# The down product of a feed-forward by token instead of by channel, with the residual, the last norm and the output in the same order

## The chip, the cores and the metric

The kernel runs on one core of one Trainium2 chip. The metric is the device time of one execution in microseconds, as the median of several runs. The engines are TensorE (PE; its weight loads are PEld), VectorE (DVE), ScalarE (ACT), GpSimd (POOL) and SyncE (SP), whose queue issues nearly all DMAs. All arithmetic is float32; products of matrices are made from high and low parts in float32r.

## The reference

Two transformer blocks of 256 tokens and 1024 channels follow each other. The first has a convolution, a differential attention and a mixture of 32 experts, the second four mixers, a cross attention to a memory and a feed-forward with a short convolution. What concerns the change is the end:

```python
def conv_ffn(xn, w_up, w_conv, w_down):
    u = causal_depthwise_conv(xn @ w_up, w_conv)
    a, g = jnp.split(u, 2, axis=-1)
    return (a * jax.nn.silu(g)) @ w_down
...
        h = h + conv_ffn(rms_norm_2(h, g_ffn[l]), w_up[l], w_ffconv[l], w_down[l])
    return rms_norm_2(h, g_final)
```

`rms_norm_2` divides each token by the root of the mean square over its channels and multiplies by a gain for each channel. `w_up` is 1024 x 5632, `w_down` 2816 x 1024; 2816 is 22 blocks of 128 (`NFF`).

## The kernel before

The residual stream `xT` lies in SBUF with channels in the partitions: 8 tiles of 128 channels by 256 tokens. Weights come from HBM in loads of 1 MB into slots of 8 KB a partition (21 in all) and are split, block by block, into a high part (ScalarE, L364) and a low part (VectorE, L367). A product is then three (`mm3`, L453 to L458): high by high, high by low, low by high. Blocks are used in one written order (`self.blocks`), split up to `AHEAD` + 1 = 4 blocks ahead and loaded up to 12 loads ahead. The program is issued in the order of the Python code (`manual_schedule`): work beside the main run of products stands in generators (`spawn`), each of which takes a step whenever `tick` is called after a block.

The feed-forward (`feed_forward`, L1982) goes over the 22 blocks j. `raise_` (L2021) makes the two up products of block j, 24 products of 256 columns each. `gated` (L1994) then scales by the norm, convolves, gates and splits the result into high and low parts, in steps. `lower` (L2031) makes the down product of block j - 5 (`LAG`): the weights are the stationary operand, the gated values of 256 tokens the moving one, for each of 8 tiles of 128 output channels. The sums over all blocks stay in four PSUM banks (`acc`), two tiles to a bank. The last two blocks are taken together, tile by tile, so that `residual` (L2054) can add tiles to `xT` and square them while others are still being summed. Behind the last product come the sums of squares over the partitions as products with a column of ones (`stat`, L418), three Newton steps for the reciprocal root (`rsqrt`, L401), a diagonal matrix of it (L432) and a product with ones that spreads it to all partitions (L2083), then the multiplication of the output (L2085) and four stores from SP's queue (L2086). The gain has been put in before by ScalarE (L2080). The output is written as channels by tokens and transposed on the host.

Products with 512 moving columns exist elsewhere: `projN` (L492) has the activations of 128 tokens as stationary operand and 512 columns of weights moving, with the same `mm3`. Transposes on TensorE exist too (L1664 and others).

## Time and profile before

| | |
|---|---|
| runs, us | 1077.84, 1075.33, 1077.87; median 1077.84 |
| the profiled execution | span 1075.6 us, 2.2 under the median; the profile gives no other time for it |
| TensorE busy | 917.5 us (85%) |
| VectorE, ScalarE busy | 517.0 us (48%), 341.5 us (32%) |
| DMA | 301.14 MB, mean 280 GB/s |
| chain that ended last | PE 39%, DMA 38% (the experts' weights), DVE 2%, ACT 1% |
| feed-forward's down products | 528 of the 6250 products |

A busy share is taken over the whole span, and the stages differ: the experts' stage in the middle follows the loads, the stages before and after follow TensorE. Matmuls overlap in the profile, so the time of a product in a run of them is the distance from start to start and not its duration. The granted clock is the TensorE clock that the chip allows, as a share of full speed.

### The profile page before, as it was taken

Reading aid. Unit: us, or ns where it says so; the run is one execution under the profiler, and the core shown is the slowest. Engines: PE = TensorE matmul, PEld = TensorE weight load, DVE = VectorE, ACT = ScalarE, POOL = GpSimd, SP = SyncE. Lnnn points to the kernel's source line nnn. Section 1 sums busy time; section 2 is a strip of 40 time slices with the busy share of each in tenths; the row PEclk is TensorE's granted clock in tenths of the full one; section 3 lists DMA queues with packets and bytes.
Section 4 is the critical chain, followed back from the end, with each engine's and each line's share of the span. In section 5 each row is a group of like instructions: output and inputs, shape, how many; then the busy total and the mean of one; then the engine's idle time right before and its main releaser. Section 6 shows DMA issues by size and latency. Waiting matters only on the chain.

```text
span 1075.6 us, 15338 instructions
## 1 busy us (share of the span) xinstructions
PE 917.5 (85%) x6250; PEld 657.8 (61%) x6251; DVE 517.0 (48%) x1144; ACT 341.5 (32%) x614; POOL 1.2 (0%) x12
## 2 busy tenths in 40 slices
PE   6989989978766867667766995999999999999996
PEld 6759989734220403122210730688899899999995
DVE  6999978501110100001010020648486489878885
ACT  5326555201020101000000011554464465544453
POOL 0000000000000000000000000000000000000000
PEclk9999999989696878787796997998999999999998
DMA  9726556859999999999999999942365295453001
GB/s 368 294 78 232 201 191 248 301 225 420 420 418 420 421 420 418 420 420 419 419 420 421 420 418 422 394 161 100 119 211 184 90 363 209 169 185 118 2 1 40
DMA packets 45006, 301.14 MB, mean 280 GB/s; under 512 B 4864, under 2 KB 8320, under 8 KB 9088
## 3 DMA queue, kind: packets, MB, share of 16 engines
q1 hardware_dynamic: 44640, 299.58, 70.4%
q8 instruction: 51, 0.84, 0.3%
q10 hardware_dynamic: 288, 0.50, 0.2%
q14 instruction: 27, 0.22, 0.1%
HBM read 299.02 MB, written 1.05 MB: 279 GB/s over the span
## 4 chain that ended last, share of the span: by engine, by line
PE 39%; DMA 38%; DVE 2%; ACT 1%; issue 0%; DVEq 0%; SPq 0%; ACTq 0%
DMA slot<-in_we_dram 38%; PE ps L456 10%; PE ps L457 10%; PE ps L458 10%; PE ps L467 1%; PE ps L1384 1%; PE ps L1473 1%; PE ps L1956 1%; PE ps L1505 1%; PE ps L1922 1%; PE ps L1489 0%; PE ps L1738 0%; DVE slot L367 0%; PE ps L1735 0%; PE ps L420 0%
## 5 line engine op out<-in xcount | busy, mean ns | idle before, releaser
L456 PE MATMUL ps<-slot,slot 128*128 128x256 f32 (+1 forms) x1020 | 304.9, 299 | 0.4 <-DVE k L1797 0.4
L457 PE MATMUL ps<-slot,slot 128*128 128x256 f32 (+1 forms) x1020 | 297.6, 292 | 0.8 <-DVE slot L367 0.8
L458 PE MATMUL ps<-slot,slot 128*128 128x256 f32 (+1 forms) x1020 | 297.3, 292 | 0.2 <-DVE slot L367 0.2
L1505 PE MATMUL ps<-slot,k 128*32 128x512 f32 x1024 | 171.6, 778 | 77.5 <-DMA slot<-in_we_dram 77.5
L456 PEld LDWEIGHTS ps<-slot,slot 128*128 128x128 f32 x1020 | 196.6, 193 | 11.8 <-issue 7.3
L457 PEld LDWEIGHTS ps<-slot,slot 128*128 128x128 f32 x1020 | 196.8, 193 | 5.5 <-DVE slot L367 1.8
L367 DVE TENSOR_TENSOR slot<-slot,slot 128x1024 fp32r<-128x1024 f32 x159 | 191.9, 1217 | 14.2 <-ACT slot L364 14.2
L458 PEld LDWEIGHTS ps<-slot,slot 128*128 128x128 f32 x1020 | 196.7, 193 | 3.1 <-DVE slot L367 0.4
L364 ACT ACTIVATE slot<-slot 128x1024 fp32r<-128x1024 f32 x159 | 163.6, 1047 | 23.7 <-PE ps L458 17.7
L1505 PEld LDWEIGHTS ps<-slot,k 128*32 128x32 f32 x1024 | 26.3, 121 | 213.2 <-DMA slot<-in_we_dram 176.9
L1489 PE MATMUL ps<-slot,k 128*32 128x512 f32 x512 | 64.9, 627 | 33.2 <-DMA slot<-in_we_dram 27.4
L1544 DVE TENSOR_TENSOR xT<-xT,ps 128x512 f32<-128x512 f32 x28 | 19.2, 687 | 118.3 <-PE ps L1542 118.3
L1513 DVE TENSOR_TENSOR k<-k,ps 128x512 f32<-128x512 f32 x8 | 5.5, 687 | 133.0 <-PE ps L1505 133.0
L1475 ACT ACTIVATE k<-ps 128x512 f32<-128x512 f32 x16 | 9.6, 597 | 173.7 <-PE ps L1473 173.7
L1489 PEld LDWEIGHTS ps<-slot,k 128*32 128x32 f32 x512 | 13.6, 111 | 76.7 <-DMA slot<-in_we_dram 40.8
L1512 DVE SCALAR_TENSOR_TENSOR k<-k,ps 128x512 f32<-128x512 f32 x8 | 5.5, 687 | 113.9 <-ACT k L1511 113.9
L1473 PEld LDWEIGHTS ps<-k,slot 128*128 128x128 f32 x256 | 38.8, 243 | 27.2 <-issue 25.2
L1473 PE MATMUL ps<-k,slot 128*128 128x128 f32 x256 | 40.4, 330 | 16.3 <-DVE k L1406 8.6
L705 DVE SCALAR_TENSOR_TENSOR slot<-slot,params,slot 128x256 f32<-128x256 f32 x120 | 51.5, 477 | 0.0
L456 PE MATMUL ps<-k,slot 128*128 128x256 f32 x176 | 49.8, 283 | 0.0
L457 PE MATMUL ps<-k,slot 128*128 128x256 f32 x176 | 49.8, 283 | 0.0
L458 PE MATMUL ps<-k,slot 128*128 128x256 f32 x176 | 49.8, 283 | 0.0
(337 smaller groups left out, 931.3 us busy)
## 6 DMA issues: line engine op xcount, KB each, us to landing
slot<-in_we_dram SPq DMA_DIRECT2D x192, 1024.0 KB, 19.9
slot<-in_w_dram SPq DMA_DIRECT2D x47, 1024.0 KB, 5.2
slot<-in_wup_dram SPq DMA_DIRECT2D x22, 1024.0 KB, 5.3
slot<-in_wdn_dram SPq DMA_DIRECT2D x11, 1024.0 KB, 4.9
slot<-in_wkv_dram SPq DMA_DIRECT2D x8, 1024.0 KB, 19.9
xT<-in_xT_dram SPq DMA_DIRECT2D x2, 512.0 KB, 5.9
slot<-in_w_dram SPq DMA_DIRECT2D x2, 512.0 KB, 7.6
slot<-in_mem_dram SPq DMA_DIRECT2D x1, 1024.0 KB, 5.0
```

The costliest lines, as they stand in the source:

```text
L364: self.nc.scalar.activation(hi, w, AF.Copy)
L367: self.nc.vector.tensor_tensor(lo, w, hi.bitcast(F32), OP.subtract)
L456: mm(out, l[0], r[0], start=start, stop=False, **kw)
L457: mm(out, l[0], r[1], start=False, stop=False, **kw)
L458: mm(out, l[1], r[0], start=False, stop=stop, **kw)
L467: self.nc.tensor.matmul(out, w[0][:, k, c], h[2][:, k, :], start=a, stop=z)
L705: stt(a, y[:, i, j : j + T], half_taps[:, i, j : j + 1], a, OP.mult, OP.add)
L1384: nc.tensor.matmul(outs[tt][:], self.mem[:, k, ts], w[0][:, j, :], **kw)
L1473: mm(pg[:, j * P : j * P + P], h2[:, tt, k * P : k * P + P], flat(oh, tt), start=tt == 0, stop=tt == 1)
L1489: mm(pd[n][32 * e : 32 * e + 32, :], hT[:, f * P + 32 * e : f * P + 32 * e + 32], t[:, 512 * e : 512 * e + 512], start=f == 0, stop=f == 3,)
L1505: mm(pgu[m][32 * e : 32 * e + 32, :], xg[k // 4][:, k % 4 * P + 32 * e : k % 4 * P + 32 * e + 32], t[:, 512 * e : 512 * e + 512], start=k ...
L1544: tt_(xflat[:, s], xflat[:, s], py[:], OP.add)
```

## The change

The down product changes its operands' roles. The gated values of 128 tokens are stationary and 512 columns of weights move; the four PSUM banks now hold two halves of tokens (`tt`) by two halves of channels (`c`). `products` makes for each block 2 x 2 triples. The residual is brought into the same order beforehand: `by_token`, spawned after the up product of block 5, transposes `xT` on TensorE in four groups of four tiles, and ScalarE copies each group into a slot (`xn`). For the last two blocks the products of token half 0 come first, then `ending(0)`, then those of half 1, then `ending(1)`. `ending` adds the residual, squares with an accumulator on ScalarE (so the sum over the channels is a number for each partition), adds two numbers, makes the Newton steps and multiplies by the reciprocal root and the gain at once. The gain is a row of 1024 in every partition now, an input of its own (`gfin`, 512 KB, loaded by SP at the start of the stage). Four stores of 256 KB go out, of each half one from SP's queue and one from ScalarE's. The output is tokens by channels; the column sums, the diagonal matrix, the spreading product and the host's transpose are gone. The rest of the diff is comments.

```diff
-        ("g_mix", 8), ("g_xa", 8), ("g_mem", 8), ("g_ffn2", 8), ("g_fin", 8), ("p_scale", 2),
+        ("g_mix", 8), ("g_xa", 8), ("g_mem", 8), ("g_ffn2", 8), ("p_scale", 2),
...
-    put("g_fin", chan(f["g_final_2"]))
...
+        "gfin": np.ascontiguousarray(np.broadcast_to(f["g_final_2"], (P, D))),
...
         xT = self.xT
         n = self.n_ffn
         h, rb = n.h, n.rb
-        acc = [self.bank() for _ in range(4)]
+        acc = [[self.bank() for _ in range(2)] for _ in range(2)]
         three = lambda a: a[:].rearrange("p (j t) -> p j t", j=2)
         fs = {}
...
                     ths.append(self.spawn(gated(j, pu), 1 if j == 0 else 0))
                 self.tick()
-        def lower(js, done=lambda i: None):
+        def take_pairs(js):
             ws, fh = [], []
             for j in js:
                 ws.append(self.next_block())
                 self.finish(ths[j])
                 fh.append(fs.pop(j))
-            for i in range(KT):
-                s = slice(i * P, i * P + P)
+            return ws, fh
+        def products(js, ws, fh, tt):
+            t = slice(tt * P, tt * P + P)
+            for c in range(2):
+                s = slice(c * 512, c * 512 + 512)
                 for j, (w, _), f in zip(js, ws, fh):
-                    self.mm3(
-                        acc[i // 2][:, i % 2 * T : i % 2 * T + T], (w[0][:, 0, s], w[1][:, 0, s]), (f[:, 0, :], f[:, 1, :]),
-                        j == 0 and i % 2 == 0, j == NFF - 1, skip_group_check=True,
-                    )
-                done(i)
-            for _, release in ws:
-                release()
+                    self.mm3(acc[tt][c][:], (f[:, 0, t], f[:, 1, t]), (w[0][:, 0, s], w[1][:, 0, s]), j == 0, j == NFF - 1)
+        def lower(j):
+            ws, fh = take_pairs([j])
+            for tt in range(2):
+                products([j], ws, fh, tt)
+            ws[0][1]()
             self.tick()
-        # the output's norm goes on beside the last products
-        total = self.t(self.sm, [P, T], "sq_sum", bufs=2)
-        st = self.bank()
-        sqs = {}
-        def residual(i):
-            if i % 2 == 0:
-                return
-            for k in (i - 1, i):
-                stt(xT[:, k, :], acc[k // 2][:, k % 2 * T : k % 2 * T + T], 0.5, xT[:, k, :], OP.mult, OP.add)
-                sqs[k] = self.k1() if k else total
-                act(sqs[k][:], xT[:, k, :], AF.Square)
-            for k in (i - 3, i - 2):
-                if k > 0:
-                    tt_(total[:], total[:], sqs[k][:], OP.add)
+        n_slot, g_slot = self.slot(), self.slot()
+        xn = n_slot[1][:].rearrange("p (a d) -> p a d", a=2)
+        gain = g_slot[1][:, :D]
+        nc.sync.dma_start(gain, self.io["gfin"])
+        def by_token():
+            for q in range(4):
+                tt, c = q // 2, 4 * (q % 2)
+                pt = self.bank()
+                for j in range(4):
+                    nc.tensor.transpose(pt[:, j * P : j * P + P], xT[:, c + j, tt * P : tt * P + P], self.ident[:])
+                yield
+                act(xn[:, tt, c * P : c * P + 512], pt[:], AF.Copy)
+                yield
+        def ending(tt):
+            ss = self.t(self.sm, [P, 2], "xmx")
+            x = xn[:, tt, :]
+            for c in range(2):
+                s = slice(c * 512, c * 512 + 512)
+                stt(x[:, s], acc[tt][c][:], 0.5, x[:, s], OP.mult, OP.add)
+                act(self.k2()[:], x[:, s], AF.Square, accum_out=ss[:, c : c + 1])
+            v = self.t(self.sm, [P, 2], "var")
+            tt_(v[:], *[ss[:, c : c + 1].to_broadcast([P, 2]) for c in range(2)], OP.add)
+            nc.vector.tensor_scalar(v[:], v[:], 1.0 / D, EPS, OP.mult, OP.add)
+            y = self.rsqrt(v[:], 2)
+            for c in range(2):
+                s = slice(c * 512, c * 512 + 512)
+                o = self.k2()
+                stt(o[:], x[:, s], y[:, 0:1], gain[:, s], OP.mult, OP.mult)
+                (nc.sync, nc.scalar)[c].dma_start(self.out[tt * P : tt * P + P, s], o[:])
         ths = []
         for j in range(NFF):
             raise_(j)
+            if j == LAG:
+                self.spawn(by_token())
             if j >= LAG:
-                lower([j - LAG])
+                lower(j - LAG)
         for j in range(NFF - LAG, NFF - 2):
-            lower([j])
-        lower([NFF - 2, NFF - 1], residual)
-        for i in (KT - 2, KT - 1, 0):
-            self.stat(st, sqs[i], i == KT - 2, i == 0)
-        out = self.out.rearrange("(i p) t -> p i t", p=P)
-        outs = []
-        for i in range(KT):
-            if i % 2 == 0:
-                outs.append(self.k2())
-            act(outs[-1][:, i % 2 * T : i % 2 * T + T], xT[:, i, :], AF.Copy, scale=self.par("g_fin", i))
-        dg = self.rstd(st, D, n.rn)
-        pb = self.bank()
-        nc.tensor.matmul(pb[:, :T], self.ones[:], dg[:], start=True, stop=True)
-        for q, o in enumerate(outs):
-            tt_(three(o), three(o), pb[:, :T].unsqueeze(1).to_broadcast([P, 2, T]), OP.mult)
-            nc.sync.dma_start(out[:, 2 * q : 2 * q + 2, :], three(o))
+            lower(j)
+        js = [NFF - 2, NFF - 1]
+        ws, fh = take_pairs(js)
+        for tt in range(2):
+            products(js, ws, fh, tt)
+            ending(tt)
 def trainium_kernel(tc, io, out, probe=None):
     with ExitStack() as ctx:
         Net(ctx, tc, io, out, probe).build()
...
         n[3:-5]: nc.dram_tensor(n, a.shape, mybir.dt.from_np(a.dtype), kind="ExternalInput").ap()
         for n, a in arrays.items()
     }
-    out = nc.dram_tensor("out_0_dram", (D, T), F32, kind="ExternalOutput").ap()
+    out = nc.dram_tensor("out_0_dram", (T, D), F32, kind="ExternalOutput").ap()
     with tile.TileContext(nc) as tc:
         trainium_kernel(tc, io, out)
     r = _run(nc, [arrays], core_ids=[0])
-    return np.ascontiguousarray(r.results[0]["out_0_dram"].T)[None]
+    return np.ascontiguousarray(r.results[0]["out_0_dram"])[None]
```

Three places show how the instructions now stand. In a row stand the line, the operation, the tile written, the tiles read (for a product the moving one first, then the stationary one) and the columns.

TensorE at the first down block, before (`k_1205` is the high and low part of the gated values, `slot_1213` the split weights, `ps_7020` to `ps_7023` the sums):

```order
L456 MATMUL ps_7020<-k_1205_7309,slot_1213_7358 128x256
L457 MATMUL ps_7020<-k_1205_7309,slot_1213_7358 128x256
L458 MATMUL ps_7020<-k_1205_7309,slot_1213_7358 128x256
L456 MATMUL ps_7021<-k_1205_7309,slot_1213_7358 128x256
L457 MATMUL ps_7021<-k_1205_7309,slot_1213_7358 128x256
L458 MATMUL ps_7021<-k_1205_7309,slot_1213_7358 128x256
```

The same place in the changed kernel, with the end of the first down block and the first group of transposes:

```order
L457 MATMUL ps_7022<-slot_1213_7359,k_1205_7310 128x512
L458 MATMUL ps_7022<-slot_1213_7359,k_1205_7310 128x512
L456 MATMUL ps_7023<-slot_1213_7359,k_1205_7310 128x512
L457 MATMUL ps_7023<-slot_1213_7359,k_1205_7310 128x512
L458 MATMUL ps_7023<-slot_1213_7359,k_1205_7310 128x512
L2065 MATMUL ps_7489<-ident,xT 128x128 x4
L456 MATMUL ps_7494<-slot_1131_6725,slot_1216_7396 128x256
```

The two operands have changed places, a product has 512 columns where it had 256, and a group of four transposes (L2065) stands between the down block and the next up product (`ps_7494`).

VectorE at the end, before: the last residuals and sums, then the Newton steps on `var`:

```order
L2058 SCALAR_TENSOR_TENSOR xT<-ps_7023,xT 128x256 x2
L2063 TENSOR_TENSOR sq_sum_7024<-sq_sum_7024,k_1377_9241 128x256
L2063 TENSOR_TENSOR sq_sum_7024<-sq_sum_7024,k_1378_9244 128x256
L427 TENSOR_SCALAR var_9286<-ps_7025 128x2
L407 TENSOR_SCALAR rs_h_1386_9288<-var_9286 128x2
L408 TENSOR_SCALAR rs_y_1387_9289<-rs_h_1386_9288 128x2
```

The same place in the changed kernel, from the last Newton step of token half 0 on:

```order
L414 SCALAR_TENSOR_TENSOR rs_y_1383_9000<-rs_t_1384_9001,rs_y_1383_9000 128x2
L2085 SCALAR_TENSOR_TENSOR k_1385_9013<-slot_1172_7024,rs_y_1383_9000,slot_1173_7025 128x512
L2085 SCALAR_TENSOR_TENSOR k_1386_9016<-slot_1172_7024,rs_y_1383_9000,slot_1173_7025 128x512
L2076 SCALAR_TENSOR_TENSOR slot_1172_7024<-ps_7022,slot_1172_7024 128x512
L2076 SCALAR_TENSOR_TENSOR slot_1172_7024<-ps_7023,slot_1172_7024 128x512
L2079 TENSOR_TENSOR var_9038<-xmx_9031 128x2
L2080 TENSOR_SCALAR var_9038<-var_9038 128x2
L407 TENSOR_SCALAR rs_h_1391_9041<-var_9038 128x2
L408 TENSOR_SCALAR rs_y_1392_9042<-rs_h_1391_9041 128x2
```

The scaled outputs of half 0 (L2085) come ahead of the residuals of half 1 (L2076), which are followed by steps of their own.

ScalarE around the first group, before (L364 is the high part of a block of weights, L1598, L2010 and L2016 belong to `gated`):

```order
L1598 ACTIVATE k_1226_7497<-k_1221_7462,params 128x256 x2
L364 ACTIVATE slot_1229_7504<-slot_1163_7010 128x1024
L364 ACTIVATE slot_1230_7538<-slot_1163_7010 128x1024
L2016 ACTIVATE k_1231_7564<-k_1225_7495 128x256
L2010 ACTIVATE k_1232_7566<-k_1226_7497 128x256
L364 ACTIVATE slot_1235_7573<-slot_1164_7012 128x1024
```

And in the changed kernel, where L2067 is the copy of a transposed group:

```order
L1598 ACTIVATE k_1226_7486<-k_1221_7463,params 128x256 x2
L364 ACTIVATE slot_1230_7498<-slot_1163_7010 128x1024
L2067 ACTIVATE slot_1172_7024<-ps_7489 128x512
L364 ACTIVATE slot_1231_7533<-slot_1163_7010 128x1024
L2017 ACTIVATE k_1232_7559<-k_1225_7484 128x256
L2011 ACTIVATE k_1233_7561<-k_1226_7486 128x256
L364 ACTIVATE slot_1237_7573<-slot_1164_7012 128x1024
L2067 ACTIVATE slot_1172_7024<-ps_7563 128x512
```

The copies stand between the high parts of the weights; the order of the others is the same.

## Rows read from the trace of the kernel before

**Rows 1.** Page, first part: busy time of TensorE, share of the span, instructions; then weight loads and others.

```profile
PE 917.5 (85%) x6250; PEld 657.8 (61%) x6251; DVE 517.0 (48%) x1144; ACT 341.5 (32%) x614; POOL 1.2 (0%) x12
```

**Rows 2.** Busy us of PE, PEld, DVE, ACT, POOL by stretch; then clock, DMA share, GB/s.

```profile
702.00:709.70 7.70, 7.70 (x35) 6.37 (x34) 5.43 (x11) 5.69 (x8) 0.00 (x0) 1.00 0.56 177
...
906.80:924.00 17.20, 17.20 (x146) 17.20 (x145) 16.05 (x28) 9.69 (x16) 0.00 (x0) 1.00 0.53 184
1045.00:1062.20 17.20, 17.20 (x145) 17.20 (x145) 12.19 (x23) 5.90 (x13) 0.00 (x0) 1.00 0.00 1
```

**Rows 3.** In order of time, PE in the last down blocks: start us, us, instruction.

```profile
1053.83 0.28 PE L457 MATMUL ps<-k,slot 128*128 128x256 f32 x1
...
1062.23 0.28 PE L458 MATMUL ps<-k,slot 128*128 128x256 f32 x1
```

**Rows 4.** In order of time, PE in the projections by token.

```profile
702.03 0.40 PE L457 MATMUL ps<-slot,slot 128*128 128x512 f32 x1
...
709.75 0.39 PE L458 MATMUL ps<-slot,slot 128*128 128x512 f32 x1
```

**Rows 5.** In order of time, PE at eight transposes behind those projections.

```profile
709.98 1.03 PE L1664 MATMUL ps<-ident,slot 128*128 128x128 f32 x8
710.77 0.48 PE L456 MATMUL ps<-slot,slot 128*128 128x512 f32 x1
711.09 0.40 PE L457 MATMUL ps<-slot,slot 128*128 128x512 f32 x1
```

**Rows 6.** In order of time, all engines: the last down blocks and the end.

```profile
1057.91 0.28 PE L458 MATMUL ps<-k,slot 128*128 128x256 f32 x1
...
1058.23 0.42 DVE L2058 SCALAR_TENSOR_TENSOR xT<-ps,xT 128x256 f32<-128x256 f32 x1 [3.01 <-PE ps L458]
...
1062.65 0.42 DVE L2058 SCALAR_TENSOR_TENSOR xT<-ps,xT 128x256 f32<-128x256 f32 x1
...
1063.16 0.42 ACT L2060 ACTIVATE k<-xT 128x256 f32<-128x256 f32 x1 [0.78 <-DVE xT L2058]
...
1065.16 0.16 DVE L427 TENSOR_SCALAR var<-ps 128x2 f32<-128x2 f32 x1 [0.91 <-PE ps L420]
...
1067.53 0.17 DVE L429 COPY rn<-rs_y 128x2 f32<-128x2 f32 x1
...
1069.52 2.48 DVE L2085 TENSOR_TENSOR k<-k,ps 128x512 f32<-128x512 f32 x4 [1.45 <-PE ps L2083]
```

**Rows 7.** Groups by line and shape: count, busy us, mean ns, idle before.

```profile
L364 ACT ACTIVATE slot<-slot 128x1024 fp32r<-128x1024 f32 x159 | 163.6, 1047 | 23.7 <-PE ps L458 17.7 <-DVE slot L367 5.2 <-DMA slot<-in_wkv_dram 0.8
...
L2060 ACT ACTIVATE k<-xT 128x256 f32<-128x256 f32 x7 | 2.7, 417 | 2.2 <-DVE xT L2058 2.2
...
L1669 ACT ACTIVATE slot<-ps 128x512 f32<-128x512 f32 x2 | 1.1, 596 | 2.2 <-PE ps L1664 2.2
...
L1512 DVE SCALAR_TENSOR_TENSOR k<-k,ps 128x512 f32<-128x512 f32 x8 | 5.5, 687 | 113.9 <-ACT k L1511 113.9
```

**Rows 8.** In order of time, ACT: an operation with an accumulator, and its reading.

```profile
836.95 0.47 ACT L1935 ACTIVATE k<-ps,xmx 128x256 f32<-128x256 f32 x1
837.31 0.20 ACT L1935 ACTIVATION_READ_ACCUMULATOR k<-ps,xmx 128x1 f32 x1
```

**Rows 9.** In order of time, PE, DVE and ACT around the first down blocks.

```profile
906.83 0.28 PE L456 MATMUL ps<-k,slot 128*128 128x256 f32 x1
...
909.39 1.22 DVE L367 TENSOR_TENSOR slot<-slot,slot 128x1024 fp32r<-128x1024 f32 x1
...
910.73 1.04 ACT L364 ACTIVATE slot<-slot 128x1024 fp32r<-128x1024 f32 x1
...
912.59 0.28 PE L456 MATMUL ps<-slot,slot 128*128 128x256 f32 x1
```

**Rows 10.** DMA issues: queue, count, KB each, median us from issue to landing.

```profile
out_dram<-k SPq DMA_DIRECT2D x4, 256.0 KB, 2.5
...
ident<-in_ident_dram ACTq DMA_DIRECT2D x1, 64.0 KB, 5.1
```

## The prediction

> **What bounds the kernel now.** I read four views in this order: the page's engine totals, the busy times by stretch with the granted clock, then TensorE's products in order of time, and last the end of the program. The totals [rows 1] name TensorE as the busiest engine, but they average over stages with different limits; the table by stretch [rows 2] decides. In the feed-forward, 906.8 to 924 and 1045 to 1062.2 for instance, TensorE is busy for all of 17.20 us at a granted clock of 1.00, the higher of its two levels, while VectorE has 16.05 us of work in the first of these stretches and 12.19 in the second. The products stand one behind the other without a hole: from 1053.83 to 1062.23 there are 70 starts, 0.120 us each [rows 3]. So whatever the change adds to or takes from TensorE's stream in this stage moves the end by as much, as long as no operand comes late. After the start of the last product come 13.37 us (1062.23 to the end of the span, 1075.6), a serial chain in which each step waits for the one before: residual on VectorE, squares on ScalarE, column sums, Newton steps on two columns, a spreading product, the output's scaling, the store [rows 6].
>
> **The products.** Each of the 22 blocks of the down product is 24 products of 256 columns (8 output tiles, 3 parts), 528 in all. The change makes 12 of 512 columns of each (2 halves of tokens, 2 of channels, 3 parts), 264 in all, with as many columns streamed. The price of such a product is in the trace, since the projections by token have the same form: 34 starts from 702.03 to 709.75 are 0.227 us each, also at clock 1.00 [rows 2, 4]. Two products of 256 take 0.240, so each pair that becomes one saves 0.013 us, and 264 x 0.013 = **3.4 us less**. The Trainium skill ("TensorE: Matmul & The Clock Gate", Back-to-back issue gap) gives the isolated spacing of warm products as N/2.4 + 2.5 ns. By that the pair would take 2 x 109.2 ns and the long product 215.8, a saving of 0.7 us in all, and the whole change would come out 0.7 us slower. The rows disagree with it at both lengths (120 and 227 ns), and the measured spacings decide.
>
> **The transposes.** The residual has to be brought into token order: 16 transposes of 128 x 128, in four groups between the blocks. Eight of the same kind took 0.79 us from 709.98 to the next product, 0.099 each, and that product held the one behind it for 0.32 us where 0.23 is usual [rows 5]. So 16 x 0.099 + 4 x 0.09 = **1.9 us more**, all of it in TensorE's stream. From below 1.6, if nothing is lost at the return to the products; from above 2.3, with the 0.120 of a product of 256 columns for each transpose [rows 3].
>
> **What lies beside other work.** Four copies of 512 columns on ScalarE (0.60 each [rows 7]) stand between the high parts of the weights; ScalarE has 9.69 us of work in 17.20 [rows 2], which covers them. If that cover goes, VectorE's low parts come late; that is a rival below. The gain is a new load of 512 KB on SP's queue, in front of the weights' loads: of the size of two output pieces, which take 2.5 us to land [rows 10], so some 2.5 to 5 us. The cover is how far the loads run ahead: from 1045 on the DMA share is 0.00 [rows 2], with six down blocks still to come. The two slots that are now held come from 21, of which the norm's pair, at most 12 loads and 4 splits use 18, so no load is issued at a later place. A block's low part is needed by its second product instead of its third, 0.227 us after the first instead of 0.240; a low part that ends at 909.39 + 1.22 = 910.61 is used from 912.59 on [rows 9], so there are 2.0 us of lead.
>
> **The end.** I count from E, the start of the last product. A residual that waits for its product starts 0.32 us after the start of that product (1057.91, 1058.23 [rows 6]), 0.04 after its 0.28 us; a product of 0.39 [rows 4] makes it 0.43. Half 0 has its last product 12 starts before E, at E - 2.72. Its second residual starts at E - 2.29 and takes 0.69 (512 columns out of PSUM [rows 7]), to E - 1.60. The square starts 0.09 later (1062.65 + 0.42 to 1063.16 [rows 6]). A square of 256 columns takes 0.42, an operation on 1024 takes 1.05, so I take 0.63 for 512, and 0.09 for reading the accumulator (836.95 to 837.51, where the operation alone is 0.47 [rows 7, 8]): E - 0.79. VectorE takes it up 0.05 later and has 13 dependent steps on two columns, 0.1975 each (from 1065.16 to 1067.53 it is 12 [rows 6]): E + 1.83. Two outputs follow at 0.62 (four took 2.48 [rows 6]): E + 3.07. Only there, in VectorE's order, stands the first residual of half 1, though its products have long been done. Its residuals and squares take until E + 5.34, the 13 steps until E + 7.91, the outputs until E + 9.22. Before, 3.6 us went by from the last output operation (1069.52 + 2.48 = 1072.00) to the end of the span; I keep them, since the last piece is again 256 KB, with a landing near 2.5 us [rows 10]. That is 12.82 us after E where 13.37 were: **0.55 us less**. What is removed from the end (column sums, diagonal, spreading product) would be worth more; the second half, serial behind the first on VectorE, takes nearly all of it back.
>
> **The sum** is -3.4 + 1.9 - 0.55 = -2.0 us, from the span of 1075.6 to 1073.6. The median of the runs is 2.2 us above that span, so it reads 1077.84 - 2.0 = **1075.8 us**, 0.19% less. A measurement of this kernel tells about 0.3%, 3.2 us, from no change, so the forecast is no change by that bound.
>
> **The rivals.**
> - *The median falls on the lower level (faster).* One of three runs before stood at 1075.33, two at 1077.8. If the changed kernel has such levels and its median takes the lower, it reads 1075.33 - 2.0 = 1073.3. At 1 in 3 a run that is 7 in 27 for a median of three; on three runs alone I take a little less.
> - *The number of weight loads sets the spacing (faster by much).* For it: the weight loads are busy 17.20 of 17.20 us, one to a product. If a load set the 0.120, a product of 512 would take 0.120 too, and 264 x 0.120 = 31.7 us would go: 1077.8 - 31.7 + 1.9 - 0.55 = 1047.5. Against it: the long products of this trace have a load each, stand at 0.227, and their loads are busy only 6.37 of 7.70 us [rows 2, 4]. The Trainium skill, same page and section, has 131 ns as the sustained spacing at 512 columns, near this rival; no row here agrees.
> - *VectorE falls behind (slower).* The place is 910 to 925, where VectorE is busy 16.05 of 17.20 us. If ScalarE reaches each copy a whole block (24 x 0.120 = 2.88 us) before TensorE has done its transposes, it stands four times, the high parts behind the copies are late, and VectorE can't make up for it; beyond its 2.0 us of lead TensorE waits 4 x 2.88 - 2.0 = 9.5 us: 1085.3. It decides from 2.0 us of holds and passes the 0.3% bound at 7.2. Against it: the first down block starts at 906.83, so the first transposes are done at about 910.2, while the high part in front of the first copy ran from 910.73 to 911.77 [rows 9]; that copy waits for nothing.
> - *ScalarE's queue stores more slowly.* The last piece goes out there. A small transfer on that queue, 64 KB, took 5.1 us to land against 2.5 for an output piece on SP's [rows 10]: 2.6 us more, 1078.4, still no change.
> - *The halves of the end overlap (faster).* If half 1 found VectorE free at E + 0.43, the same steps would end at E + 9.46 and 3.4 us more would be gained: 1072.4. VectorE's order speaks against it.
>
> **How the numbers follow.** Forecast 0.64, lower level 0.20, overlap 0.03, weight loads 0.01, slow queue 0.05, VectorE behind 0.07. Faster by over 0.3% takes the second to the fourth: 0.24. Slower takes VectorE behind, and 0.01 of the slow queue for runs that scatter upward: 0.08. The rest, 0.68, is within 0.3%. The range goes from the lower level with the cheaper transposes, 1073.0, to the slow queue with the dear ones, 1078.8; outside lie VectorE behind, overlap and weight loads, 0.11, and the scatter of the runs.
>
> **What would show it.** In the changed profile the down products should stand 0.227 us apart, a group of transposes should cost 0.4 to 0.5 us, TensorE should show no wait in the stage, the last product should start 1.5 us earlier, and the first residual of half 1 should stand right behind the outputs of half 0. The prediction is wrong if TensorE shows holes after 910, if the spacing is near 0.240 or below 0.22, or if the last store lands later than 3 us after its issue.

## The result and the profile after

The changed kernel takes 1065.14 us (median of four runs, 1064.46 to 1069.2) where the kernel before, run beside it, takes 1077.46 (1075.33 to 1077.87). The ratio is 0.9895 with a 95% interval of 0.9881 to 0.9909: 1.05% faster, over five times the forecast of 0.19%, and outside the range. The profiled execution has a span of 1067.5 us and a time of 1069.2, so 1.7 us lie around the span. It is the slowest of the four.

Where did it go? First the part that was predicted, the feed-forward. The page's first part of the changed kernel, then its busy times by stretch (busy us of PE, PEld, DVE, ACT, POOL; granted clock, DMA share, GB/s):

```profile
PE 914.1 (86%) x5988; PEld 644.2 (60%) x5989; DVE 517.3 (48%) x1146; ACT 341.7 (32%) x610; POOL 1.2 (0%) x12
```

```profile
900.00:920.00 20.00, 20.00 (x145) 18.83 (x144) 17.57 (x32) 11.87 (x20) 0.00 (x0) 1.00 0.54 200
920.00:940.00 20.00, 20.00 (x139) 18.59 (x138) 16.43 (x27) 10.36 (x17) 0.00 (x0) 1.00 0.53 169
```

TensorE is still busy all the time at a granted clock of 1.00, as in [rows 2], with 139 to 145 products in 20 us. No wait has come in. In order of time, PE in the first down block, at the first group of transposes (L2065) and behind it (start us, us, instruction):

```profile
901.00 0.40 PE L456 MATMUL ps<-slot,k 128*128 128x512 f32 x1
...
903.52 0.39 PE L458 MATMUL ps<-slot,k 128*128 128x512 f32 x1
...
903.75 0.60 PE L2065 MATMUL ps<-ident,xT 128*128 128x128 f32 x4
904.10 0.36 PE L456 MATMUL ps<-slot,slot 128*128 128x256 f32 x1
904.30 0.28 PE L457 MATMUL ps<-slot,slot 128*128 128x256 f32 x1
```

The twelve products from 901.00 to 903.75 are 0.229 us apart. Four transposes take 0.35 us to the next product, and that product holds the one behind it for 0.20 where 0.12 is usual: 0.43 for the group. The end of the program answers to [rows 6, 8]; here are PE, DVE and ACT, with the issues of the stores (SPq and ACTq):

```profile
1052.58 0.69 DVE L2076 SCALAR_TENSOR_TENSOR slot<-ps,slot 128x512 f32<-128x512 f32 x1 [0.67 <-PE ps L458]
...
1053.30 0.63 ACT L2077 ACTIVATE k<-slot 128x512 f32<-128x512 f32 x1 [0.58 <-DVE slot L2076]
...
1053.84 0.19 ACT L2077 ACTIVATION_READ_ACCUMULATOR k<-slot 128x1 f32 x1
...
1054.06 0.16 DVE L2079 TENSOR_TENSOR var<-xmx 128x2 f32<-128x2 f32 x1 [0.79 <-ACT k L2077]
...
1054.87 0.39 PE L458 MATMUL ps<-slot,k 128*128 128x512 f32 x1
...
1056.62 1.41 DVE L2085 SCALAR_TENSOR_TENSOR k<-slot,rs_y,slot 128x512 f32<-128x512 f32 x2
...
1057.95 1.28 DVE L2076 SCALAR_TENSOR_TENSOR slot<-ps,slot 128x512 f32<-128x512 f32 x2
...
1062.66 1.42 DVE L2085 SCALAR_TENSOR_TENSOR k<-slot,rs_y,slot 128x512 f32<-128x512 f32 x2
1064.11 0.35 ACTq L2086 DMA_DIRECT2D out_dram<-k  x1
```

The last product starts at E = 1054.87. Half 1's residuals (1057.95) stand right behind half 0's outputs, at E + 3.08, and the span, 1067.46 to two places, ends at E + 12.59. And the DMA issues, which answer to [rows 10] (queue, count, KB each, median us to landing):

```profile
slot<-in_we_dram SPq DMA_DIRECT2D x192, 1024.0 KB, 19.6
...
slot<-in_gfin_dram SPq DMA_DIRECT2D x1, 512.0 KB, 10.7
...
out_dram<-k SPq DMA_DIRECT2D x2, 256.0 KB, 2.0
out_dram<-k ACTq DMA_DIRECT2D x2, 256.0 KB, 2.0
```

The gain took 10.7 us to land, not 2.5 to 5, and nothing waited for it.

All of this is near the forecast, so the rest must have come from elsewhere. Landmarks show where: a line's products with count, duration ns (min/median/max), first and last start, forms. L1473 is the first line of the experts' stage, L1505 holds its last products, L1664 stands in the mixers, L1922 and L1956 in the cross attention that comes before the feed-forward. The kernel before:

```profile
L1473 PE MATMUL ps<-k,slot x256: 274/275/582, 218.8 to 596.7; 128*128 128x128 f32 x128
L1505 PE MATMUL ps<-slot,k x1024: 589/617/1063, 227.6 to 659.0; 128*32 128x512 f32 x171
L1664 PE MATMUL ps<-ident,slot x8: 270/272/273, 710.0 to 710.7; 128*128 128x128 f32 x8
L1922 PE MATMUL ps<-slot,k x32: 377/379/483, 819.1 to 838.4; 128*128 128x256 f32 x32
L1956 PE MATMUL ps<-k,slot x32: 379/379/483, 838.6 to 848.2; 128*128 128x256 f32 x32
```

The changed kernel, in a second profile (run `e7_after_again` below, span 1065.8):

```profile
L1473 PE MATMUL ps<-k,slot x256: 274/275/580, 218.9 to 589.4; 128*128 128x128 f32 x128
L1505 PE MATMUL ps<-slot,k x1024: 589/617/1062, 227.6 to 651.8; 128*32 128x512 f32 x171
L1664 PE MATMUL ps<-ident,slot x8: 271/272/273, 702.4 to 703.2; 128*128 128x128 f32 x8
L1922 PE MATMUL ps<-slot,k x32: 377/379/483, 811.6 to 830.9; 128*128 128x256 f32 x32
L1956 PE MATMUL ps<-k,slot x32: 379/379/483, 831.1 to 840.7; 128*128 128x256 f32 x32
```

The stage of the experts, from 218.8 to 659.0, was 440.2 us long and is 432.9 now: **7.3 us gone from a stage that the diff does not name**. Between L1505 and L1956 the two differ by 0.3.

In the first profile of the changed kernel the stage is 434.6 us long:

```profile
L1505 PE MATMUL ps<-slot,k x1024: 590/617/1064, 228.3 to 653.5; 128*32 128x512 f32 x171
```

That is 1.7 us more than in the second, as much as the two spans differ by; what held it up is open. The four other profiles in which the slots lie as in the changed kernel (`e1`, `e6`, `e10` and `e11` below) have 432.5 to 432.9, so the comparison goes by the second profile.

What limits that stage is in the chain that ended last, from 300 us on (start us, us, what). Before, and then the changed kernel:

```profile
307.40 19.89 DMA slot<-in_we_dram
```

```profile
307.86 19.56 DMA slot<-in_we_dram
```

A piece is the time from a load's issue to its landing, and the next load in the chain is issued right behind it. The pieces around it repeat these times to some hundredths. A stage of 440.2 us has room for 22 of them; a piece has become 0.33 us shorter, and by this estimate 22 x 0.33 = 7.3 us go. The same in the totals from 300 to 600 us, columns as above, before and changed:

```profile
300.00:600.00 300.00, 207.83 (x1226) 68.46 (x1219) 24.40 (x40) 20.03 (x36) 0.00 (x0) 0.80 1.01 420
```

```profile
300.00:600.00 300.00, 215.35 (x1262) 73.87 (x1255) 25.13 (x41) 20.36 (x38) 0.00 (x0) 0.80 1.01 427
```

The DMA engines are busy throughout in both (share 1.01), but they move 427 GB/s instead of 420. The trace's records of single packets say the same: a packet of 8 KB, the row that one partition gets from a load, took 314.9 ns on average in this stretch before and takes 309.3 now.

Two things that the diff does outside the feed-forward can reach these loads. The gain as a column group (8 columns, 32 bytes a partition) left the table `params`, and with it everything behind that table in SBUF moved down by 32 bytes: slot 0, into which the loads go, from byte 57120 of the partition (32 past a multiple of 256) to byte 57088 (a multiple of 256). And the new input `gfin` stands ahead of the weights among the inputs, so that they may lie elsewhere in HBM. Theory A takes the first, theory B the second, theory C says that runs or chips differ.

### The profile page after: what moved, and what is told of

Its sections match the earlier page's. It is cut to its first block, busy times and chain, and to the rows that moved or that the text cites. A ratio compares the mean times of both kernels' runs of the same rounds, so it can differ in the third digit from the quotient of the medians.

```text
span 1067.5 us, 14808 instructions
## 1 busy us (share of the span) xinstructions
PE 914.1 (86%) x5988; PEld 644.2 (60%) x5989; DVE 517.3 (48%) x1146; ACT 341.7 (32%) x610; POOL 1.2 (0%) x12
## 3 DMA queue, kind: packets, MB, share of 16 engines
HBM read 299.54 MB, written 1.05 MB: 282 GB/s over the span
## 4 chain that ended last, share of the span: by engine, by line
PE 38%; DMA 38%; DVE 2%; ACT 1%; issue 1%; DVEq 0%; SPq 0%; ACTq 0%
DMA slot<-in_we_dram 38%; PE ps L456 10%; PE ps L457 10%; PE ps L458 10%; PE ps L467 1%; PE ps L1384 1%; PE ps L1473 1%; PE ps L1956 1%; PE ps L1505 1%; PE ps L1922 1%; PE ps L1489 0%; PE ps L1738 0%; DVE slot L367 0%; PE ps L1735 0%; DVE k L2085 0%
## 5 line engine op out<-in xcount | busy, mean ns | idle before, releaser
L1505 PE MATMUL ps<-slot,k 128*32 128x512 f32 x1024 | 172.9, 780 | 76.4 <-DMA slot<-in_we_dram 76.4
L456 PEld LDWEIGHTS ps<-slot,slot 128*128 128x128 f32 x1020 | 196.7, 193 | 12.3 <-issue 7.3
L364 ACT ACTIVATE slot<-slot 128x1024 fp32r<-128x1024 f32 x159 | 164.4, 1049 | 50.1 <-PE ps L458 41.0
L1505 PEld LDWEIGHTS ps<-slot,k 128*32 128x32 f32 x1024 | 25.9, 121 | 214.1 <-DMA slot<-in_we_dram 179.2
L1475 ACT ACTIVATE k<-ps 128x512 f32<-128x512 f32 x16 | 9.6, 597 | 173.7 <-PE ps L1473 172.5
L1473 PEld LDWEIGHTS ps<-k,slot 128*128 128x128 f32 x256 | 40.2, 251 | 27.1 <-issue 25.0
L1473 PE MATMUL ps<-k,slot 128*128 128x128 f32 x256 | 41.8, 339 | 16.3 <-DVE k L1406 8.6
L1511 ACT ACTIVATE k<-ps 128x512 f32<-128x512 f32 x8 | 4.8, 597 | 126.4 <-PE ps L1505 126.4
L456 PE MATMUL ps<-slot,k 128*128 128x512 f32 (+1 forms) x96 | 36.8, 383 | 0.0
L457 PE MATMUL ps<-slot,k 128*128 128x512 f32 (+1 forms) x96 | 36.7, 382 | 0.0
```

The lines of the kernel that those rows point to most:

```text
L364: self.nc.scalar.activation(hi, w, AF.Copy)
L456: mm(out, l[0], r[0], start=start, stop=False, **kw)
L457: mm(out, l[0], r[1], start=False, stop=False, **kw)
L1473: mm(pg[:, j * P : j * P + P], h2[:, tt, k * P : k * P + P], flat(oh, tt), start=tt == 0, stop=tt == 1)
L1505: mm(pgu[m][32 * e : 32 * e + 32, :], xg[k // 4][:, k % 4 * P + 32 * e : k % 4 * P + 32 * e + 32], t[:, 512 * e : 512 * e + 512], start=k ...
```

## The experiments

**One tile moved, in the kernel before.** Run `e1_before_shift32`.

```diff
-        self.slots = pool("slots", 1)
+        self.slots = pool("slots", 1); self.late = pool("late", 1)
...
-        nc.scalar.activation(self.cp.tile([P, 1], F32, name="warm")[:], self.ones[:, :1], AF.Copy)
+        nc.scalar.activation(self.late.tile([P, 1], F32, name="warm")[:], self.ones[:, :1], AF.Copy)
```

> The kernel before, with nothing of the change in it; only one small tile (4 bytes a partition, which takes 32) is moved from ahead of the slots to behind them, so that scratch tiles and all 21 slots begin 32 bytes earlier: slot 0 at byte 57088 of the partition, a multiple of 256, as in the changed kernel, instead of 57120. Theory A (the gain of the experts' stage comes from where the slots begin): the loads of 1 MB go at 427 GB/s instead of 420, 2.456 us instead of 2.497 each, and 200 of them give 8.2 us: 1077.5 - 8.2 = 1069.3, ratio 0.992, packets of 8 KB at a median of 309 ns instead of 314. Theory B (it comes from where the inputs lie in HBM, which the new input and the narrower gain table shift): nothing changes, 1077.5, 314 ns. Theory C (the chip or the run differed): 1077.5 within 0.2%, and the rate need not follow the address.

Measured: 1069.19 us, ratio 0.9914 (0.9894 to 0.9934), a gain of 8.4 us without any of the change's instructions. Packets took 309.3 ns, the experts' stage 432.9 us (218.7 to 651.6):

```profile
L1473 PE MATMUL ps<-k,slot x256: 274/275/582, 218.7 to 591.6; 128*128 128x128 f32 x128
L1505 PE MATMUL ps<-slot,k x1024: 589/617/1063, 227.3 to 651.6; 128*32 128x512 f32 x171
...
300.00:600.00 300.00, 211.73 (x1226) 73.59 (x1227) 24.98 (x41) 19.43 (x35) 0.00 (x0) 0.80 1.01 427
```

Theory A gave 1069.3. Theories B and C gave no gain.

**The slots alone moved up, in both kernels.** Run `e3_after_shift_up32` puts the changed kernel's slots back to 57120; `e2_before_shift_up32` has the same edit in the kernel before, and `e5_before_shift_up96` has 24 columns in place of 8.

```diff
-        self.slots = pool("slots", 1)
+        self.pad = pool("pad", 1).tile([P, 8], F32, name="pad"); self.slots = pool("slots", 1)
```

> The changed kernel, with an unused tile of 32 bytes a partition ahead of the slots alone, which puts slot 0 back at 57120, where the kernel before has it; inputs, scratch tiles and instructions are those of the changed kernel. Theory A: the gain of the loads is gone again, packets at 314 ns, 420 GB/s, and what is left is the feed-forward's own, which was forecast at 2.0 us: 1075.5, ratio 0.998. If the scratch tiles' places make part of the gain, less comes back. Theory B: 1065.1, ratio 0.989, as the changed kernel. Theory C: no bound.

Measured: 1074.4 us, ratio 0.9974 (0.9961 to 0.9987). Packets are back at 314.9 ns and the rate at 420 GB/s:

```profile
300.00:600.00 300.00, 210.63 (x1229) 73.56 (x1221) 24.42 (x40) 20.12 (x37) 0.00 (x0) 0.79 1.01 420
```

The gain of the loads is gone with 32 bytes in front of the slots, while inputs and scratch tiles stay where the change put them. Theory B gave 1065.1 and is out. What is left, 0.26% (0.13 to 0.39) or 3.2 us between the medians, lies near the 0.19% forecast for the feed-forward, but that is luck and no measure of it. The profiles of the two kernels (1074.9 and 1075.6), both with the fall of the clock that comes below, are only 0.7 us apart, mainly because the down products stand wider apart in this run (last section). And four of its six times lie 2.1 to 2.8 us below the profiled one, as times without that fall would.

> The kernel before, with an unused tile of 32 bytes a partition ahead of the slots alone: slot 0 at 57152, a multiple of 64 and of 128 but 64 past a multiple of 256; everything else lies where it lay. Theory A with a boundary of 64 bytes: the whole gain, 8.2 us, 1069.3, packets at 309 ns. Theory A with a boundary of 256 bytes: no gain, 1077.5, packets at 314 ns. Theories B and C: 1077.5.

> The kernel before, with an unused tile of 96 bytes a partition ahead of the slots alone: slot 0 at 57216, 128 past a multiple of 256. Rows of 8 KB took 314.9 ns in the experts' stage where slots begin at 32 past a multiple of 256, 313.9 at 64 past, and 309.3 at a multiple. If only multiples of 256 count: 313.9 ns again, 421 GB/s, and 1074.3 to 1077.5. If multiples of 128 do: 309.3 ns, 427 GB/s, 1069.3. Theory B (the inputs' places in HBM): 314.9 ns and 1077.5.

Measured: 1074.33 us (ratio 0.9971, 0.9959 to 0.9982) at 64 past a multiple of 256, and 1071.87 (0.9946, 0.9928 to 0.9963) at 128 past. Packets took 313.9 ns in both, the rate was 421 GB/s. So of the offsets tried (0, 32, 64 and 128) only the multiple of 256 gives the full rate; 64 or 128 give 1.0 ns of the 5.6. That multiple, 57088, is not one of 512. The Trainium skill ("DMA: Bandwidth & Descriptors", How a descriptor splits into AXI transactions) has a rule of this form for what a descriptor reads: it goes in transactions of 256 bytes, and where it does not start at a multiple of 256, its first transaction starts at the boundary below. An estimate by that rule of the Trainium skill: a row of 8 KB takes 33 transactions where 32 would do, whether it lies 32, 64 or 128 past. The runs agree in that only the multiple of 256 is free; here it is the place that is written which was moved, and the price is 1.5 to 1.8% of a row of 8 KB. They also show something that the rule does not have, the small difference between 32 and 64. Why an offset costs time is not shown by the runs, and neither is whether the destination counts alone or its place against the source, which no run varied on purpose.

The times of these two runs are lower than their rates explain. The experts' stage gave 1.7 and 2.1 us (438.5 and 438.1), not 3.3 and 6.5. Two further differences are in their profiles. One is the down products' own spacing, of which more below. The other is the clock, in 730 to 760 us, where TensorE is nearly always busy: first the kernel before, then `e5_before_shift_up96` (columns as above).

```profile
730.00:760.00 30.00, 29.58 (x189) 25.47 (x188) 21.88 (x69) 11.40 (x24) 0.69 (x5) 0.89 0.21 71
```

```profile
730.00:760.00 30.00, 29.57 (x217) 25.38 (x217) 21.77 (x68) 13.09 (x29) 0.69 (x5) 1.00 0.31 106
```

At a mean granted clock of 0.89, that is with part of the stretch at the lower level of 1.2 GHz, 189 products start, at 1.00 it is 217. From L1664 to L1922 the profiles with the fall take 109.1 us (710.0 to 819.1 above) and those without 106.2 (707.9 to 814.1 in `e5_before_shift_up96`; for the changed kernel in `e11_after_third`, below). It is 3 us by one event, in some executions of a kernel and not in others. A profile with half the fall, `e9_shift_half_rows` with 0.94 in this stretch, lies between with 107.6. With slots at a multiple of 256 it is there in `e1_before_shift32` and not in `e11_after_third`; with slots at 32 past it is there in the kernel before and not in `e4_before_input_only`. So it does not go with the address. Times that differ by 3 us can't be compared before one knows on which side of it they lie.

**The inputs alone.** Run `e4_before_input_only`.

```diff
         "ident": np.eye(P, dtype=np.float32),
+        "gfin": np.ascontiguousarray(np.broadcast_to(f["g_final_2"], (P, D))),
```

> The kernel before, with the new input of 512 KB among its inputs, at the same place in their order, and never read: in HBM the weights come behind it, in SBUF nothing moves. Theory A: 1077.5, packets at 314 ns. Theory B: the gain of the experts' stage, 6 to 10 us, 1067.5 to 1071.5, packets at 309 ns. Theory C: 1077.5 within 0.2%.

Measured: 1078.04 us, ratio 1.0004 (0.9990 to 1.0017), packets at 314.9 ns:

```profile
300.00:600.00 300.00, 212.46 (x1231) 71.89 (x1222) 24.42 (x40) 20.18 (x38) 0.00 (x0) 0.77 1.01 419
```

Theory B falls here from the other side too.

**Is the price paid by the row or by the byte?** Runs `e9_shift_half_rows` (on top of the moved tile) and `e8_before_half_rows` (on the kernel before) cut each load of the experts' weights in two.

```diff
-        if key == ("w1", 0):
+        if key == ("w1", 0) or key[0] == "e":
             for c in (slice(0, 1024), slice(1024, 2048)):
                 self.nc.sync.dma_start(s[1][:, c], src[:, c])
```

> The kernel before moved by 32 bytes (slots at a multiple of 256), and each of the 192 loads of the experts' weights cut into two of 512 KB, whose rows are 4 KB long instead of 8. It is the measure for its twin with the slots at 32 past a multiple of 256, to come. If a packet costs by its bytes alone, 309.3 / 2 = 154.7 ns and 1069.2 as with whole rows; if there is a cost for each packet besides, it shows here as more than 154.7 ns.

> The kernel before, slots at 32 past a multiple of 256 as it has them, with each of the 192 loads of the experts' weights cut into two of 512 KB, whose rows are 4 KB long. Its twin with slots at a multiple of 256 took 159.2 ns for such a packet and 1077.3 us. Whole rows of 8 KB lost 5.6 ns a packet by the offset (314.9 against 309.3). If the offset costs once for each packet, whatever its length: 164.8 ns here, 3.5% more than the twin, so some 15 us more in the experts' stage of 440.9 us: 1092. If it costs by the byte: 162.0 ns, 1.8%, some 8 us: 1085. If only whole rows of 8 KB suffer: 159.2 ns and 1077.3.

Measured: with slots at a multiple of 256 1077.33 us (0.9991, 0.9979 to 1.0004) and 159.2 ns for a packet of 4 KB; at 32 past 1086.68 us (1.0099, 1.0076 to 1.0121) and 163.1 ns. Rates of both, the aligned one first:

```profile
300.00:600.00 300.00, 257.30 (x1225) 71.26 (x1218) 24.44 (x40) 20.04 (x36) 0.00 (x0) 1.00 1.03 420
```

```profile
300.00:600.00 300.00, 250.85 (x1172) 64.22 (x1164) 23.65 (x39) 18.07 (x32) 0.00 (x0) 1.00 1.03 409
```

The offset costs 3.9 ns for a row of 4 KB and 5.6 for one of 8 KB, between the two forecasts (5.6 and 2.8). It grows with the length, but by less than in proportion, so shorter rows lose more: 2.4% of 159.2 against 1.8% of 309.3. Neither theory of the price holds as written. The aligned pair shows a price of every packet besides: a straight line through 159.2 and 309.3 gives 150.1 ns for 4 KB and, as an estimate, 9.1 ns for a packet. Halving the rows cost as much as misplacing them. The two lines also bear out that the loads set this stage: TensorE's granted clock is 1.00 in them, where it was 0.80 with whole rows, and the rate of the loads did not rise.

**The changed kernel again.** Runs `e7_after_again` and `e11_after_third`, no edit.

> The changed kernel as it is, beside the others on this chip: 1065.1 within 0.2%, ratio 0.989. With the kernel before moved by 32 bytes, which ran at 1069.2 (ratio 0.9914), the difference is the feed-forward's own share, which was forecast at 2.0 us, 0.19%.

> The changed kernel as it is, as the measure for the joint end beside it: 1065 to 1066, ratio 0.988 to 0.990, with executions in which the granted clock falls around 740 to 755 us some 3 us above those in which it stays.

Measured: 1065.94 us (0.9885, 0.9863 to 0.9906) and 1064.8 us (0.9890, 0.9874 to 0.9907). The first profile has the fall of the clock (span 1065.8), the second has not (1063.1, and 106.2 us from L1664 to L1922):

```profile
L1664 PE MATMUL ps<-ident,slot x8: 271/272/273, 702.7 to 703.5; 128*128 128x128 f32 x8
L1922 PE MATMUL ps<-slot,k x32: 377/379/483, 808.9 to 828.2; 128*128 128x256 f32 x32
```

With the 1.7 us around the span the second gives 1064.8, the median of its runs. So the median of the changed kernel seems to lie with executions without the fall. The profile before has the fall, and its 1075.6 and 1.7 give 1077.3, near the medians of the kernel before. The cleanest measure of the feed-forward alone is the profile of `e1_before_shift32` (span 1067.6) beside the one of `e7_after_again` (1065.8): both have the slots at a multiple of 256 and the fall of the clock, and they are 1.8 us apart where 2.0 were forecast.

**Another end.** Runs `e6_after_one_end` and `e10_after_one_end_again` (the same kernel) ask whether the end could be shorter: one chain of Newton steps for both halves, and the outputs of half 0 on ScalarE.

```diff
-        def ending(tt):
-            ss = self.t(self.sm, [P, 2], "xmx")
+        ss = self.t(self.sm, [P, 4], "mx")
+        def residual(tt):
...
+            if tt == 0:
+                gained.extend(self.k2() for _ in range(2))
+                for o, s in zip(gained, half):
+                    tt_(o[:], x[:, s], gain[:, s], OP.mult)
+        def ending():
...
+            sv = ss[:].rearrange("p (t c) -> p t c", c=2)
+            tt_(v[:], sv[:, :, 0], sv[:, :, 1], OP.add)
...
+            for c, s in enumerate(half):
+                act(gained[c][:], gained[c][:], AF.Copy, scale=y[:, 0:1])
+                nc.sync.dma_start(self.out[0:P, s], gained[c][:])
+                o = xn[:, 1, s]
+                stt(o, o, y[:, 1:2], gain[:, s], OP.mult, OP.mult)
+                (nc.sync, nc.scalar)[c].dma_start(self.out[P : 2 * P, s], o)
...
             products(js, ws, fh, tt)
-            ending(tt)
+            residual(tt)
+        ending()
```

> The changed kernel with another end: the sums of squares of both halves go into one tile, and one chain of Newton steps serves both; the residual of half 0 is multiplied by the gain while half 1 is still being summed, so that ScalarE writes the outputs of half 0 beside VectorE, which writes those of half 1. From the start E of the last product: the gain's two products fill VectorE up to about E - 0.2, two residuals up to E + 1.2, square and sum up to E + 2.0 (1.48 from the start of the second residual, as in half 0 of the changed kernel), Newton steps of 2.56 up to E + 4.5, two outputs on each engine up to E + 5.9 where the changed kernel has E + 9.2. Theory D (the chain of the second half behind the first on VectorE is what the end costs): 3.3 us less than the changed kernel, 1061.8, ratio to before 0.986. Rival E (the end is set by the stores, 3.4 us from the last output, which now come four at a time): the gain is 2 us or less, 1063 or more.

> The changed kernel with the joint end once more, for a closer measure beside the changed kernel on the same chip. In the profile its end took 10.55 us from the start of the last product instead of 12.6; 3.3 us came off VectorE's chain, and 1.2 went back to the stores. So 2.0 us less than the changed kernel, 0.19%.

In order of time in the first of these runs (span 1063.3), all engines, from the last product on:

```profile
1052.79 0.39 PE L458 MATMUL ps<-slot,k 128*128 128x512 f32 x1
...
1054.75 0.16 DVE L2086 TENSOR_TENSOR var<-mx 128x2 f32<-128x2 f32 x1 [0.85 <-ACT k L2077]
...
1057.32 1.33 ACT L2090 ACTIVATE k<-k,rs_y 128x512 f32<-128x512 f32 x2 [2.60 <-DVE rs_y L414]
1057.32 1.42 DVE L2093 SCALAR_TENSOR_TENSOR slot<-slot,rs_y,slot 128x512 f32<-128x512 f32 x2
...
1058.98 0.41 SPq L2091 DMA_DIRECT2D out_dram<-k  x1
```

The outputs end at 1058.74, E + 5.95, as worked out: 3.3 us came off the chain, and theory D is right on VectorE's order. But the span ends 4.6 us later, where the changed kernel needs 3.4 from its last output: four stores of 256 KB that leave within 1 us give 1.2 us back, so rival E holds for the stores. The end takes 10.55 us instead of the 12.6 in all three profiles of the changed kernel. In the time of the whole kernel this is not resolved: 1064.45 (0.9874, 0.9857 to 0.9892) and 1064.58 (0.9885, 0.9869 to 0.9902) stand beside 1065.94 and 1064.8 of the changed kernel. The medians are 1.5 and 0.2 us apart where 2.0 were expected, and the intervals overlap. In the profile of the second run the experts' stage began at 220.8 us instead of 218.9, so the front of the program scatters by as much as the end gained. The version is not measurably slower or faster than the changed kernel, and faster than the kernel before.

## Why the prediction was wrong

**The step that failed** is in "What lies beside other work". It counted the load of the gain, the slots that are held and the places in the order of the loads, and from "no load is issued at a later place" it took everything ahead of the feed-forward as unchanged. The one line of the diff that removes the gain's 8 columns from the table got no term. It moved the destination of every load by 32 bytes, and in a stage of 440 us that is bound by its loads this was worth 7.3 us in the traces and 8.4 us in the run that has this alone. The first paragraph had narrowed the view to the feed-forward because the change stands there. The page's chain, with 38% on the experts' loads, was in the table of the profile and was not asked what could make those loads faster.

Between profiles that both have the fall of the clock (the kernel before and `e7_after_again`), the difference of 9.8 us is made up of: experts' stage -7.3; from there to the feed-forward -0.3; L1956's last product to the last down product -1.54 (1062.23 - 848.2 = 214.03 before, 1053.19 - 840.7 = 212.49 after); the end -0.76 (13.37 to 12.61); the front +0.1. The last product of `e7_after_again`:

```profile
1053.19 0.39 PE L458 MATMUL ps<-slot,k 128*128 128x512 f32 x1
```

The end before is itself not the same in every profile: it takes 13.05 us in `e1_before_shift32` and 13.72 in `e2_before_shift_up32`, so its share is known to some 0.3 us. The medians differ by 12.3. The 2.5 us between fit the fall of the clock, 3 us, which most executions of the changed kernel seem to miss. That is argued and not shown: it rests on three profiles of the changed kernel, two with the fall and one without, and on how the medians lie to their spans. Why the fall comes or stays away, and whether the change has a part in it, is open.

**The products**: -3.4 forecast. The spacing is 0.2286 us over all 246 pairs of neighbours in the trace that do not stand right behind transposes, not 0.227, so 264 x (0.240 - 0.2286) = 3.0. **The transposes**: +1.9 forecast; four groups at 0.43 are 1.7, and the stage as a whole needs 1.54 less, so that they cost about 1.5. The two errors cancel: -1.5 net was forecast, -1.54 measured. The rival by which the number of weight loads sets the spacing is out. What the Trainium skill ("TensorE: Matmul & The Clock Gate", Back-to-back issue gap) gives at 512 columns, 215.8 ns as an estimate by its formula or 131 ns sustained, is not what the changed kernel shows either, with 228.6.

**The end**: -0.55 forecast. By the profile after: second residual of half 0 at E - 2.29 (forecast E - 2.29), first sum at E - 0.81 (E - 0.74), outputs from E + 1.75 (E + 1.83), residuals of half 1 at E + 3.08 (E + 3.07), last output done at E + 9.21 (E + 9.22), end of the span at E + 12.59 (E + 12.82). The chain is right to 0.1 us at every step, in part by small errors that cancel: two outputs were counted at 1.24 us and took 1.33 to the next operation, and the last step of the forecast, from E + 7.91 to E + 9.22, is 1.31 where two outputs at 0.62 make 1.24. Added up as written the end would have been 12.75 and its gain 0.62. The landing was the term that was off, 3.4 us instead of 3.6. The slow ScalarE queue did not show: 2.0 us on either queue. VectorE did not fall behind; TensorE has no wait after 910.

**The levels of the median** were a rival at 0.20, and something of it seems to have happened. Its two levels, 2.5 us apart, fit the fall of the clock around 745 us, 3 us, which the profile before shows and other profiles do not; the run at 1075.33 has no trace that could show it.

So the feed-forward is worth 1.8 to 2.3 us in the traces, by the kernel before that is compared, and 2.0 by the forecast, less than the 3.2 us that the prediction took as the bound of no change. The result passes that bound because of an address.

## What to carry to other kernels

In a stage that is bound by DMA, let the destination in SBUF begin at a multiple of 256 bytes: at 32, 64 or 128 past it, rows of 8 KB took 1.5 to 1.8% longer here, and rows of 4 KB at 32 past 2.4%. Anything that changes the size of an earlier tile moves the later ones, so print the addresses of both versions before you take a stage as untouched. And when a local change moves the time by more than its stage could give, compare landmarks from stage to stage before explaining anything in the stage itself.

## What the runs showed that was not expected

- The spacing of down products depends on where the slots lie against the scratch tiles. In the kernel before it is 0.120 us [rows 3], also with both kinds of tile moved by 32. With the slots alone moved up by 32 it is 0.1183: 77 starts in order of time on PE in `e2_before_shift_up32`, the first and the last.

```profile
1048.81 0.28 PE L457 MATMUL ps<-k,slot 128*128 128x256 f32 x1
...
1057.80 0.28 PE L458 MATMUL ps<-k,slot 128*128 128x256 f32 x1
```

  In the changed kernel, where the slots' weights are the moving operand, the same move makes it worse: 0.2332 instead of 0.2286 over all pairs in `e3_after_shift_up32`. In the first case the slots came to a multiple of 64 and the scratch tiles stood 32 past one, in the second the other way round. These 528 x 0.0017 = 0.9 and 264 x 0.0046 = 1.2 us come near the 1.1 us less and 1.2 us more that the feed-forwards of these two profiles take against their own kernels. Why the places matter there is open.
- The granted clock fell to 0.89 over 730 to 760 us in some executions and cost 3 us. In the profile of the kernel before, TensorE had been busy at 1.00 for all of 700 to 740 us and then stood for 0.42 us just before the fall; profiles without the fall have the same break.
- A packet has a price of its own beside its bytes, 9.1 ns by the estimate from rows of 4 and 8 KB. Whether rows of 16 KB would give another 1.5% to this stage was not tried.
